# A 90-degree rotation by 128x128 transposes: first loads into the output buffers, narrower macro tiles at both ends

## The chip, the cores and the metric

The kernel runs on one core of one Trainium2 chip. The metric is the device time of one execution in microseconds (us), lower is better; the time before is the median of three runs. Separately, one execution was recorded by the hardware profiler: its page and its trace are what the text reads.

## The reference

```python
"x": np.random.randn(8192, 8192).astype(np.float32), "k": 1
def reference(x, k):
    return np.rot90(x, k)
```

With k = 1 the output is `out[M-1-c, r] = x[r, c]`: each column of the input becomes a row of the output, and the last column becomes the first row. Nothing is computed. 268.4 MB are read and 268.4 MB are written.

## The kernel before, in words

The input is cut into bands of R = 1024 rows (`for r0`), each band into two macro tiles of C = 4096 columns (`widths` returns `[M // 2] * 2`), so there are 16 macro tiles of 16 MB. A macro tile is handled in two stages.

**Load stage.** For each of the 8 row tiles `t` of 128 rows, SyncE's queue (SP) issues one load of 128 rows by 4096 columns, 2 MB, into a buffer `a` (line 82); each partition gets one row piece of 16 KB. The pool of `a` has two buffers. VectorE (DVE) then copies the row tile into eight chunks `ar` of 128x512 (line 89); the copy turns the order of the columns inside each block of 128 around. The pool of `ar` has 68 buffers: one macro tile needs 64 of them, so the next macro tile's copies can take 4 at once and the others as they come free. DVE takes them in the order of the loads, and the buffer `a` can be loaded again when its eight copies are done.

**Store stage.** For each group of G = 4 blocks of 128 columns, which is one chunk column, TensorE (PE) transposes the blocks of all 8 row tiles into PSUM (line 104), two column blocks to a PSUM tile `ps` of 128x2048, of which there are two. ScalarE (ACT) copies each `ps` into one half of an output buffer `o` (line 109), two halves to a buffer, and then issues one store of 2 MB (line 115): 128 partitions of 16 KB, each written as four pieces of 4 KB, one in each of four blocks of 128 output rows. The pool of `o` has two buffers as well. A group can only start when all 8 row tiles of the macro tile have been loaded and copied, since each of its output rows runs over all 1024 input rows of the band.

The engines each go through their instructions in a fixed order, and a framework sets that order and the semaphores. Loads are on SP's DMA queue, stores on ACT's; both queues use the same 16 DMA engines. A step waits for the data and the buffer that it needs, and a DMA also for the earlier one that used the same of eight completion semaphores. `whole_reads`, run at the end of the build, joins a contiguous DMA source that stands as four pieces into one run; it acts on the stores of `o`, and stays as it is.

In the text L0 to L127 are the loads and S0 to S127 the stores, in order. Before, macro tile n has loads and stores 8n to 8n+7.

Of the kernel before, what the change touches and what calls it, by code (L numbers as in the profile page):

```python
# [2 lines left out]

# [5 lines left out]

P = 128  # L10

R = 1024
RT = R // P
CH = 512
G = 4
PW = 2


def whole_reads(nc):

    for fn in nc.m.functions:
        for block in fn.blocks:  # L30
            for n, ins in enumerate(block.instructions):
                if not isinstance(ins, mybir.InstDMACopy):
                    continue
                src = ins.ins[0]
                ap = [list(d) for d in src.ap]
                if len(ap) == 3 and ap[2][0] == 1 and ap[1][0] == ap[2][1]:
                    ap = [ap[0], [1, 1], [1, ap[1][1] * ap[2][1]]]
                    block.instructions[n] = copy.replace(
                        ins,
                        ins=[copy.replace(src, ap=ap)],  # L40
                        ant_dge_precooked=False,
                    )


def widths(first, last, M):

    return [M // 2] * 2


@with_exitstack  # L50
def kernel(
    ctx: ExitStack,
    tc: tile.TileContext,
    x: bass.AP,
    k: bass.AP,
    out: bass.AP,
):
    nc = tc.nc
    assert k == 1, f"only k=1 supported, got {k}"
    nc.at_finalize(whole_reads)  # L60

    N, M = x.shape
    dt = x.dtype

    consts = ctx.enter_context(tc.tile_pool(name="consts", bufs=1))
    ident = consts.tile([P, P], dt)
    make_identity(nc, ident)

    a_pool = ctx.enter_context(tc.tile_pool(name="a_pool", bufs=2))
    r_pool = ctx.enter_context(tc.tile_pool(name="r_pool", bufs=68))  # L70
    o_pool = ctx.enter_context(tc.tile_pool(name="o_pool", bufs=2))
    psum_pool = ctx.enter_context(
        tc.tile_pool(name="psum", bufs=2, space=bass.MemoryType.PSUM)
    )

    for r0 in range(0, N, R):
        c0 = 0
        for C in widths(r0 == 0, r0 + R == N, M):
            chunks = {}
            for t in range(RT):  # L80
                a = a_pool.tile([P, C], dt, tag="a")
                nc.sync.dma_start(  # L82
                    out=a[:], in_=x[r0 + t * P : r0 + (t + 1) * P, c0 : c0 + C]
                )


                for j in range(C // CH):
                    ar = r_pool.tile([P, CH // P, P], dt, tag="ar")
                    nc.vector.tensor_copy(  # L89
                        out=ar[:],  # L90
                        in_=a[:, j * CH : (j + 1) * CH].rearrange(
                            "r (b m) -> r b m", m=P
                        )[:, :, ::-1],
                    )
                    chunks[t, j] = ar

            for g0 in range(0, C // P, G):
                o = o_pool.tile([P, G, R], dt, tag="o")
                for h in range(0, G, PW):
                    ps = psum_pool.tile([P, PW, R], mybir.dt.float32)  # L100
                    for w in range(PW):
                        g = g0 + h + w
                        for t in range(RT):
                            nc.tensor.transpose(  # L104
                                ps[:, PW - 1 - w, t * P : (t + 1) * P],
                                chunks[t, g * P // CH][:, g % (CH // P), :],
                                ident,
                            )
                    nc.scalar.copy(o[:, G - PW - h : G - h, :], ps[:])  # L109

                top = M - c0 - (g0 + G) * P
                dst = out[top : top + G * P, r0 : r0 + R].rearrange(
                    "(g m) f -> m g f", g=G
                )
                nc.scalar.dma_start(out=dst, in_=o[:])  # L115
            c0 += C


# [1 line left out]
_INS = ['x', 'k']  # L120
_OUTS = [((8192, 8192), 'float32')]

_NUMBERS = {'k': 1}


# [26 lines left out]
```

## Time and profile before

| | |
|---|---|
| median of 3 runs | 1278.4 us (1276.62 to 1279.38) |
| the profiled execution's own time | 1282.29 us |
| its span, first to last instruction | 1280.5 us |
| PE busy | 720.3 us, 56% |
| ACT busy | 467.0 us, 36% |
| DVE busy | 355.2 us, 28% |
| DMA over the span | 537.55 MB, 420 GB/s on average |
| loads (line 82) | 128 of 2048 KB, 16.6 us from issue to landing |
| stores (line 115) | 128 of 2048 KB, 15.9 us from issue to landing |

The page cuts the span into 40 slices of 32 us; a digit in it is the busy share in tenths, and the row GB/s what the DMA engines moved. "Idle before" in the list of groups is the time in which an engine waited just ahead of that instruction, with what ended the wait. The chain is the work that ended last, followed back from the end. The profiled execution took 3.9 us more than the median of the runs.

### The profile page before, as it was taken

What the parts mean: (1) busy time and instruction counts of PE and PEld (TensorE: products, weight loads), DVE (VectorE), ACT (ScalarE), POOL (GpSimd) and SP (SyncE); (2) the same over time, 40 slices, a digit from 0 to 9 for tenths busy, and PEclk for the clock granted to TensorE, in tenths of its full rate; (3) what the DMA queues carried; (4) which work ended last, traced back from release to release, by engine and by line L of the source; (5) the groups of instructions that cost most, each with busy time, mean ns of one, the idle gap of its engine ahead of it and who ended that gap; (6) DMA issues with size and microseconds to landing.
All of it is one profiled execution on the core that took longest, in us unless ns stands there. A gap on an engine that the chain in (4) does not pass through costs nothing.

```text
span 1280.5 us, 10385 instructions
## 1 busy us (share of the span) xinstructions
PE 720.3 (56%) x4096; PEld 686.7 (54%) x4096; DVE 355.2 (28%) x1024; ACT 467.0 (36%) x257; POOL 0.7 (0%) x6
## 2 busy tenths in 40 slices
PE   0445555655665456565655655656556655655574
PEld 0345555655555456555555654555555645555474
DVE  3432223222322232233223222322232223222300
ACT  0233334333333343343334333433343334333455
POOL 0000000000000000000000000000000000000000
PEclk9967867687777877768677677686776777787778
DMA  9999999999999999999999999999999999999988
GB/s 346 364 421 425 426 426 424 429 429 428 429 430 427 430 425 431 425 431 427 426 428 429 430 422 426 428 428 426 429 429 424 425 426 426 428 426 427 427 352 357
DMA packets 36913, 537.55 MB, mean 420 GB/s; under 512 B 4096, under 2 KB 4096, under 8 KB 4096
## 3 DMA queue, kind: packets, MB, share of 16 engines
q1 hardware_dynamic: 18432, 268.44, 49.9%
q10 hardware_dynamic: 18432, 268.44, 49.4%
q8 instruction: 32, 0.52, 0.2%
q14 instruction: 17, 0.14, 0.0%
HBM read 268.44 MB, written 268.44 MB: 419 GB/s over the span
## 4 chain that ended last, share of the span: by engine, by line
DMA 79%; ACT 18%; PE 1%; DVE 1%; issue 1%; ACTq 0%; SPq 0%
DMA out_dram<-o 76%; ACT o L109 18%; DMA a<-in_x_dram 3%; PE ps L104 1%; DVE ar L89 1%; ACTq L115 0%; ACTq L109 0%; SPq L82 0%
## 5 line engine op out<-in xcount | busy, mean ns | idle before, releaser
L104 PE MATMUL ps<-ident,ar 128*128 128x128 f32 x4096 | 720.3, 358 | 548.6 <-ACT o L109 502.3
L104 PEld LDWEIGHTS ps<-ident,ar 128*128 128x128 f32 x4096 | 686.7, 192 | 581.9 <-ACT o L109 532.6
L109 ACT COPY o<-ps 128x2048 f32<-128x2048 f32 x256 | 465.7, 1871 | 805.3 <-DMA out_dram<-o 750.7
L89 DVE COPY ar<-a 128x512 f32<-128x512 f32 x1024 | 355.2, 422 | 871.5 <-DMA a<-in_x_dram 871.5
L109 ACT ACT_TABLE_LOAD x1 | 1.3, 1283 | 0.7 <-PEq L133 0.7
masks.py:199 POOL TENSOR_SCALAR_AFFINE_SELECT ident<-ident 128x128 f32<-128x128 f32 x1 | 0.3, 293 | 0.1
masks.py:197 POOL MEMSET ident<- 128x128 f32 x1 | 0.2, 204 | 0.3 <-POOLq L133 0.3
L133 POOL MEMSET const-bfloat16-1.0<- 128x1 bf16 x1 | 0.1, 101 | 0.0
L133 POOL MEMSET const-uint8-127<- 128x1 uint8 x1 | 0.1, 101 | 0.0
L133 POOL MEMSET const-float32-0.0<- 128x1 f32 x1 | 0.1, 98 | 0.2 <-issue 0.2
L133 POOL MEMSET const-float32-1.0<- 128x1 f32 x1 | 0.1, 98 | 0.0
## 6 DMA issues: line engine op xcount, KB each, us to landing
a<-in_x_dram SPq DMA_DIRECT2D x128, 2048.0 KB, 16.6
out_dram<-o ACTq DMA_DIRECT2D x128, 2048.0 KB, 15.9
```

Of the source, the lines that this page charges most:

```text
L89: nc.vector.tensor_copy(out=ar[:], in_=a[:, j * CH : (j + 1) * CH].rearrange("r (b m) -> r b m", m=P)[:, :, ::-1],)
L104: nc.tensor.transpose(ps[:, PW - 1 - w, t * P : (t + 1) * P], chunks[t, g * P // CH][:, g % (CH // P), :], ident,)
L109: nc.scalar.copy(o[:, G - PW - h : G - h, :], ps[:])
L133: nc = _bacc.Bacc("TRN2", target_bir_lowering=False, num_devices=1)
```

## The change

1. The macro tiles are made by `macro_tiles`. The widths stay 4096 except in two places: the first macro tile of the first band becomes three of 1024, 1024 and 2048 columns, and the last of the last band becomes three of 2048, 1024 and 1024 columns.
2. A load stays 2 MB: for a macro tile of width C it takes q = 4096 // C row tiles at once, so that each partition gets q row pieces of C elements (4 of 4 KB for C = 1024, 2 of 8 KB for C = 2048). DVE's copies go through the row tiles of a load, and inside each through its chunks; their number and shapes are the same.
3. The first two loads, L0 and L1, take their buffers from the pool of `o` in place of that of `a`. They are the whole first macro tile of 1024 columns. SP so issues four loads ahead of its first wait, and a wait for DVE's copies stands ahead of the first eviction into each of those two buffers.
4. The last group of the last macro tile stores each half, 1 MB, after its own eviction; all other groups store 2 MB as before.

The stores have the same shape and the same groups of four blocks otherwise. SP's loads become 4 of 4x1024, 4 of 2x2048, 112 of 4096, 4 of 2x2048 and 4 of 4x1024 elements per partition; the counts of PE's, DVE's and ACT's compute instructions don't change.

```diff
-def widths(first, last, M):
-
-    return [M // 2] * 2
+def macro_tiles(N, M):
+
+    for r0 in range(0, N, R):
+        widths = [W] * (M // W)
+        if r0 == 0:
+            widths[:1] = [1024, 1024, 2048]
+        if r0 + R == N:
+            widths[-1:] = [2048, 1024, 1024]
+        c0 = 0
+        for C in widths:
+            yield r0, c0, C
+            c0 += C
...
-            for t in range(RT):
-                a = a_pool.tile([P, C], dt, tag="a")
-                nc.sync.dma_start(
-                    out=a[:], in_=x[r0 + t * P : r0 + (t + 1) * P, c0 : c0 + C]
-                )
+        q = W // C
+        chunks = {}
+        for t0 in range(0, RT, q):
+            if loads < 2:
+                a = o_pool.tile([P, W], dt, tag="o")
+            else:
+                a = a_pool.tile([P, W], dt, tag="a")
+            loads += 1
+            a = a.rearrange("r (q c) -> r q c", q=q)
+            nc.sync.dma_start(
+                out=a,
+                in_=x[r0 + t0 * P : r0 + (t0 + q) * P, c0 : c0 + C].rearrange(
+                    "(q r) c -> r q c", q=q
+                ),
+            )
+            for u in range(q):
                 for j in range(C // CH):
...
-                        in_=a[:, j * CH : (j + 1) * CH].rearrange(
+                        in_=a[:, u, j * CH : (j + 1) * CH].rearrange(
...
-                    chunks[t, j] = ar
+                    chunks[t0 + u, j] = ar
...
+            S = PW if last and g0 + G == C // P else G
...
+                done = h + PW
+                if done % S == 0:
+                    top = M - c0 - (g0 + done) * P
+                    dst = out[top : top + S * P, r0 : r0 + R].rearrange(
+                        "(g m) f -> m g f", g=S
+                    )
+                    nc.scalar.dma_start(
+                        out=dst, in_=o[:, G - done : G - done + S, :]
+                    )
```

More of the change, by code (lines that the diff above doesn't have):

```diff
@@ L16 @@
 RT = R // P
+W = 4096
 CH = 512
@@ L74 @@
     )
[L76 to L79, printed above, removed]
-            for t in range(RT):
-                a = a_pool.tile([P, C], dt, tag="a")
-                nc.sync.dma_start(
-                    out=a[:], in_=x[r0 + t * P : r0 + (t + 1) * P, c0 : c0 + C]
-                )
+    tiles = list(macro_tiles(N, M))
+    loads = 0
+    for r0, c0, C in tiles:
+        last = (r0, c0, C) == tiles[-1]
+        q = W // C
[14 more added lines that the diff above has]
+            for u in range(q):
                 for j in range(C // CH):
@@ L94 @@
                     )
-                    chunks[t, j] = ar
[L97 to L116, printed above, removed]
+                    chunks[t0 + u, j] = ar
+        for g0 in range(0, C // P, G):
+            ot = o_pool.tile([P, W], dt, tag="o")
+            o = ot.rearrange("m (g f) -> m g f", g=G)
+            S = PW if last and g0 + G == C // P else G
+            for h in range(0, G, PW):
+                ps = psum_pool.tile([P, PW, R], mybir.dt.float32)
+                for w in range(PW):
+                    g = g0 + h + w
+                    for t in range(RT):
+                        nc.tensor.transpose(
+                            ps[:, PW - 1 - w, t * P : (t + 1) * P],
+                            chunks[t, g * P // CH][:, g % (CH // P), :],
+                            ident,
+                        )
+                nc.scalar.copy(o[:, G - PW - h : G - h, :], ps[:])
+                done = h + PW
[6 more added lines that the diff above has]
+                        out=dst, in_=o[:, G - done : G - done + S, :]
+                    )
 _INS = ['x', 'k']
```

## The prediction

> **What bounds the kernel now.** I read the page's slices and chain first, then the busy table by stage, then the order of time at both ends.
>
> ```profile
> DMA  9999999999999999999999999999999999999988
> GB/s 346 364 421 425 426 426 424 429 429 428 429 430 427 430 425 431 425 431 427 426 428 429 430 422 426 428 428 426 429 429 424 425 426 426 428 426 427 427 352 357
> ...
> DMA 79%; ACT 18%; PE 1%; DVE 1%; issue 1%; ACTq 0%; SPq 0%
> ```
>
> The DMA engines are full everywhere, and no compute engine is over 56% busy. In the middle they move 427 GB/s; only the first two and last two slices of 32 us fall to about 355. So the middle is at its limit, and only the ends can be won. The table by stage (us, busy by engine, clock, DMA share, GB/s) puts sizes on that:
>
> ```profile
> 0.00:3.00 3.00, 0.00 (x0) 0.00 (x0) 0.00 (x0) 1.28 (x1) 0.70 (x6) 1.00 0.43 98
> 3.00:12.00 9.00, 0.66 (x2) 0.29 (x2) 2.77 (x8) 0.00 (x0) 0.00 (x0) 1.00 1.01 431
> 12.00:50.00 38.00, 4.14 (x12) 1.74 (x12) 16.65 (x48) 0.00 (x0) 0.00 (x0) 1.00 0.92 338
> ...
> 500.00:1220.00 720.00, 417.12 (x2345) 399.78 (x2344) 202.60 (x584) 265.46 (x146) 0.00 (x0) 0.75 1.01 427
> 1224.00:1234.00 10.00, 8.15 (x51) 7.92 (x52) 2.70 (x8) 7.09 (x4) 0.00 (x0) 0.67 0.62 264
> 1234.00:1270.00 36.00, 25.71 (x208) 23.85 (x205) 0.00 (x0) 22.45 (x13) 0.00 (x0) 0.95 0.89 375
> 1270.00:1280.50 10.50, 0.00 (x0) 0.00 (x0) 0.00 (x0) 3.00 (x2) 0.00 (x0) 0.57 0.75 317
> ```
>
> Each stage loses its length times (1 - rate/427). Front: 2.3 us before data flows, 7.9 in 12 to 50, about 1 more up to 80. Back: 3.8 + 4.4 + 2.7 = 10.9. Some 22 us in all, no more than that is in reach. Note 3 to 12: with two loads queued, loads alone reach 431. From 12 on each new load waits for a buffer to land and be copied. DVE's copies, in order of time, are the landings:
>
> ```profile
> 8.18 2.77 DVE L89 COPY ar<-a 128x512 f32<-128x512 f32 x8 [8.18 <-DMA a<-in_x_dram]
> ...
> 13.05 2.77 DVE L89 COPY ar<-a 128x512 f32<-128x512 f32 x8 [2.09 <-DMA a<-in_x_dram]
> ...
> 50.54 2.77 DVE L89 COPY ar<-a 128x512 f32<-128x512 f32 x8 [2.65 <-DMA a<-in_x_dram]
> ```
>
> The second load lands 4.87 us after the first, the next six need (50.54 - 13.05)/6 = 6.25 us each. At 427 GB/s a 2 MB transfer costs 4.91. A load with no store beside it, in the two-buffer rhythm, wastes about 1.38 us. At the other end the last seven stores are issued from 1237.97 to 1273.03, 5.84 us apart: 0.93 wasted each.
>
> **What the skill says.** (1) "DMA: Bandwidth & Descriptors", Issuing engines are not separate DMA queues: SP's and ACT's transfers share the same 16 engines. The trace agrees: mixed, each queue gets a transfer through every 9.8 us, half rate. (2) Same page, Queues, rings and completion order: an engine takes turns between queues packet by packet. The trace has whole 16 KB rows on the load side and equal shares; it can't show turns with 4 KB pieces. (3) Same page, Why small descriptors are slow: about 3 cycles per packet on beats of 32 B. (4) Same page, Latency and other measured facts: large power-of-two row pitches can cost HBM copies half their rate. The stores already write pieces 4 MiB apart (128 rows of 32 KB), within a mix at 427.
>
> **The change, part by part.**
>
> *Four loads at the start.* SP issues L0 to L3 without a wait. DMA keeps the 427 GB/s of the deep queue until about 2.3 + 4 x 4.91 = 22 us, in place of 12. Two more loads at 4.87 in place of 6.25: **-2.8 us**. The added waits: ACT's first eviction into each output buffer waits for DVE's copies of L0 and L1 (done about 11.0 and 15.8); behind that wait are only ACT's table load, 1.3 us, and evictions that have no data before 15.5. Nothing is late.
>
> *Narrow macro tiles in front.* S0 needs L0 and L1 only. Before, the last chunk it needed was ready at 50.98 and S0 was issued at 57.06, 6.1 later. Now that chunk is the seventh copy of L1, 13.05 + 7 x 0.35 = 15.5, so S0 is issued at about 21.6, 35 us sooner. But that is not 35 us won. A 4096-wide tile needs eight loads landed before its first store; in a mix, loads and stores go one to one, so the lead of loads over stores has to grow from 2 (first tile) through 4 to 8, in stretches with loads alone. My walk, at 9.8 per pair: S0 to S3 mix with L4 to L7 from 23 to 62; L7's copies and the 6.1 us path put S4's data at about 73, so 62 to 73 is loads alone (L8, most of L9); S4 to S7 mix until about 112; then loads alone to L15's landing at about 126, and S8 is issued at about 132.5. From there it is the old kernel at 57.06 with eight pairs done. Eight pairs at 9.83 (110 evictions from 142.69 to 1223.72) are 78.6, so the old S0 corresponds to 135.7: about 3.2 gained, the four-load part included. By count: before, 2 fast loads and 7 slow ones alone; now 4 fast ones, and about 5 slow. The first load of each new stretch alone may already be queued and so go at 4.9: at most 2 x 1.38 more. On the low side, if stores get the larger share against narrow loads, S3 is done 9 us sooner and two more loads stand alone: 2 x 1.38 less. I take **-3.0** for the front, range -0.2 to -5.8.
>
> *Narrow macro tiles at the back.* In the last band loads run eight ahead already, since that is what the tile before needs. L127 lands at about 1223.9, and S120's first eviction at 1229.35 waits for PE, whose transposes start at 1225.64 because ACT released a PSUM tile at 1225.6, not because of L127's chunk (ready about 1224.4). A tile that needs fewer loads so releases nothing: **0**. If narrow loads lag behind stores, the mix lasts longer and up to four of the last stores run at 4.91 instead of 5.84: 4 x 0.93 = 3.7 gained; if they lag so far that a store group waits for its loads, one 6.1 us path is exposed. Both ends go to the range.
>
> *Split last store.* The last 2 MB store is issued at 1273.03. Its first half could be issued about 1.9 us (one eviction) sooner. The one before, issued at 1266.89, fills the engines until about 1271.8 to 1273.5 (shortest issue to landing 6.6, of which 4.9 is data), so only the gap of about 1.7 between it and the last one's first packet can close; the extra issue on ACT holds the second eviction up 0.7. **-1.0**, between 0 and -2.4.
>
> *Narrow loads.* Sixteen of 128. By (3), 16 KB in four packets takes 4 x 131 cycles against 515, 1.7%; in two, 0.6%: at 4.91 each, 8 x 0.083 + 8 x 0.03 = 0.9, an estimate. The stores with their 4 KB pieces hold 427 beside loads, and up to 419 alone. **+0.4**, from 0 to 0.9, except as in the third rival. SP's issue, 0.33, may become the 0.55 that the four-piece stores take: hidden behind 5 us and more of queued data.
>
> Sum: -3.0 + 0 - 1.0 + 0.4 = **-3.6 us**. The profiled execution of 1282.3 would become 1278.7, its span 1276.9; from the median of 1278.4, **1274.8**.
>
> **The rivals.**
>
> *More is won at the back (1270.3).* Turns by packet let stores run ahead of narrow loads; the lead falls before loads end, and four store-only transfers join the mix (-3.7), with the gap at 1224 to 1234 partly filled (-0.8). For it: 264 GB/s there. Against: the equal halves of the trace, and a 4 KB-piece store counted like a 16 KB load.
>
> *The stretch is only moved (1277.4).* The lead of eight must be built anyway. If stores take the larger share in front, the two loads gained stand alone later, and only the split is left: -1.0.
>
> *Slower: reads of pieces 4 MiB apart (1286.8).* If reads suffer from that pitch as (4) tells, at its 164 against 214 GB/s a 4.91 us load takes 1.5 more; eight loads of four pieces make +12 against -3.6, about +8.4. It decides against me from (3.6 + 2.6)/16 = 0.4 us per narrow load. Against: the stores' same pattern at full rate, and neighbouring partitions only 32 KB apart. That the change doesn't do what it says is excluded: the order of instructions has four loads ahead of SP's first wait.
>
> **How the numbers follow.** 0.2% is 2.6 us, about what a measurement of this kernel tells from no change. Forecast 0.53 (1272 to 1277.5), more at the back 0.14, only moved 0.22, slower reads 0.11. Faster by over 0.2%: most of the forecast (0.47), the first rival (0.14), little of the second (0.02): 0.63. Slower: 0.11. Same: 0.26. The range leaves out the slow rival and the far end of the first: 1270.0 to 1279.5, where the upper end is the second rival with half of the narrow loads' and the share's cost on top.
>
> **What would show it.** Landings of L0 to L3 about 4.9 apart; the first store issued near 21.6; two stretches of loads alone near 62 to 73 and 112 to 135 at about 340 GB/s; S8 issued near 132.5; the last seven full stores still some 5.8 apart; 427 GB/s in between. Wrong it would be if L2 and L3 land over 5.5 apart (narrow reads cost), if S0 to S3 take well under 9.8 each beside narrow loads (turns by packet), or if stores at the end go faster than 5.8 apart.

## The result and the profile after

The changed kernel took 1277.56 us (median of 4 runs, 1276.9 to 1278.14) beside 1278.89 for the kernel before: a ratio of 0.9993 with a 95% interval of 0.9975 to 1.001. That is 0.9 us faster, from 3.2 faster to 1.3 slower. Measured once more with 21 runs, the unaltered changed kernel came to 1278.06 beside 1279.98, ratio 0.9986 (0.9979 to 0.9993): 1.8 us faster, and clear of zero. The forecast was 3.6 us. Its sign held, its size was twice what was found.

The profiled executions differ by more than that: spans of 1280.5 before and 1275.1 after. Single executions of one kernel scatter by some us here (1276.19 to 1283.31 in 37 runs of the kernel before), and the profiled one of before (1282.29) lies 2.0 to 3.9 above the medians of its sets of runs. So the traces are read for where time goes within one execution, and the runs for how much it is.

The slices of the changed kernel's page, with its DMA packets:

```profile
DMA  9999999999999999999999999999999999999998
GB/s 362 427 403 399 421 422 425 429 430 429 428 429 430 429 429 420 428 429 430 427 428 430 431 427 429 427 426 429 427 430 428 428 425 430 426 424 424 420 408 340
DMA packets 41153, 537.55 MB, mean 422 GB/s; under 512 B 4112, under 2 KB 4112, under 8 KB 8208
```

Before, the second slice had 364; now it has 427, but the third and fourth fell to 403 and 399, which were at 421 and 425. The loss was moved and spread as well as cut. And 4096 packets of 2 to 8 KB are new: eight narrow loads of 4x1024 elements, each cut into 512 packets of 4 KB.

The busy table of the changed kernel by finer stages (us, busy by engine, clock, DMA share, GB/s):

```profile
3.00:20.00 17.00, 8.34 (x32) 5.51 (x32) 6.83 (x20) 2.96 (x2) 0.00 (x0) 1.00 1.02 411
...
23.00:26.00 3.00, 2.18 (x16) 1.52 (x14) 2.17 (x7) 3.00 (x2) 0.00 (x0) 1.00 1.03 302
26.00:30.00 4.00, 2.95 (x25) 2.71 (x25) 0.60 (x2) 0.39 (x1) 0.00 (x0) 1.00 0.99 356
30.00:58.00 28.00, 7.01 (x36) 6.16 (x36) 5.55 (x16) 7.27 (x4) 0.00 (x0) 0.67 1.01 429
...
62.00:66.00 4.00, 0.54 (x2) 0.25 (x3) 1.82 (x6) 0.00 (x0) 0.00 (x0) 0.50 0.90 326
...
114.00:134.00 20.00, 8.42 (x43) 7.07 (x43) 9.45 (x28) 3.73 (x2) 0.00 (x0) 0.55 0.93 378
```

Against 428 GB/s, each line loses its length times (1 - rate/428): 0.7 us at the start, where narrow loads go at 411 with full engines (wide ones went at 431); 0.9 + 0.7 from 23 to 30, around the first store; nothing in the mix of 30 to 58; 1.0 and 2.3 in the two stretches of loads alone. With what lies between, and 2.5 before data flows, the front loses about 9.4 us; before it was 11.2.

DVE's copies of the changed kernel in order of time are the landings of L1 to L7:

```profile
13.61 2.77 DVE L111 COPY ar<-a 128x512 f32<-128x512 f32 x8 [2.34 <-DMA a<-in_x_dram]
18.72 2.77 DVE L111 COPY ar<-a 128x512 f32<-128x512 f32 x8 [2.34 <-DMA a<-in_x_dram]
23.82 2.77 DVE L111 COPY ar<-a 128x512 f32<-128x512 f32 x8 [2.33 <-DMA a<-in_x_dram]
35.12 2.77 DVE L111 COPY ar<-a 128x512 f32<-128x512 f32 x8 [8.52 <-DMA a<-in_x_dram]
47.68 2.77 DVE L111 COPY ar<-a 128x512 f32<-128x512 f32 x8 [9.78 <-DMA a<-in_x_dram]
60.50 2.77 DVE L111 COPY ar<-a 128x512 f32<-128x512 f32 x8 [10.05 <-DMA a<-in_x_dram]
65.45 2.77 DVE L111 COPY ar<-a 128x512 f32<-128x512 f32 x8 [2.18 <-DMA a<-in_x_dram]
```

ACT's evictions in the same stretch show when S0 and S1 had landed (the first two lines: each waits for a store), and when S4 and S8 could start and were issued:

```profile
36.71 3.63 ACT L133 COPY ot<-ps 128x2048 f32<-128x2048 f32 x2 [10.32 <-DMA out_dram<-ot]
...
44.32 3.64 ACT L133 COPY ot<-ps 128x2048 f32<-128x2048 f32 x2 [3.98 <-DMA out_dram<-ot]
...
69.50 3.76 ACT L133 COPY ot<-ps 128x2048 f32<-128x2048 f32 x2 [21.54 <-PE ps L128]
73.28 0.55 ACTq L141 DMA_DIRECT2D out_dram<-ot  x1
...
130.20 3.79 ACT L133 COPY ot<-ps 128x2048 f32<-128x2048 f32 x2 [31.03 <-PE ps L128]
134.01 0.55 ACTq L141 DMA_DIRECT2D out_dram<-ot  x1
```

L0 to L3 land 5.1 apart (forecast 4.9). Beside the stores, L5 and L6 need 12.6 and 12.8 us while the two stores land 7.6 apart; equal halves would be 9.8 each. A third of the engines would be 3 x 4.91 = 14.7, two thirds 7.4. S4 was issued at 73.28 (the forecast's first stretch of loads alone ended at about 73), S8 at 134.01 (forecast 132.5).

The last band. Before, DVE's copies for L126 and L127, the last two in order of time:

```profile
1214.13 2.77 DVE L89 COPY ar<-a 128x512 f32<-128x512 f32 x8 [7.07 <-DMA a<-in_x_dram]
1223.92 2.77 DVE L89 COPY ar<-a 128x512 f32<-128x512 f32 x8 [7.02 <-DMA a<-in_x_dram]
```

In the changed kernel, the landings of L124 to L127:

```profile
1206.42 2.78 DVE L111 COPY ar<-a 128x512 f32<-128x512 f32 x8 [7.09 <-DMA a<-in_x_dram]
1214.55 2.77 DVE L111 COPY ar<-a 128x512 f32<-128x512 f32 x8 [5.35 <-DMA a<-in_x_dram]
1232.91 2.77 DVE L111 COPY ar<-a 128x512 f32<-128x512 f32 x8 [15.59 <-DMA a<-in_x_dram]
1249.48 2.77 DVE L111 COPY ar<-a 128x512 f32<-128x512 f32 x8 [13.80 <-DMA a<-in_x_dram]
```

ACT's evictions and issues there, in order of time, from the eviction for S118 on:

```profile
1196.33 3.64 ACT L133 COPY ot<-ps 128x2048 f32<-128x2048 f32 x2 [3.88 <-DMA out_dram<-ot]
1206.40 0.55 ACTq L141 DMA_DIRECT2D out_dram<-ot  x1
1207.05 3.63 ACT L133 COPY ot<-ps 128x2048 f32<-128x2048 f32 x2 [7.07 <-DMA a<-in_x_dram]
```

L126 and L127 need 18.4 and 16.6 us; before, every load took 9.8, and L127 landed at 1223.92, with S119 to S127 still to be issued. Now only S124 to S127 are issued after it. But S118, evicted at 1199.97, is issued at 1206.40, just as L124 lands: in the trace both carry the same completion semaphore, number 109. For 6.4 us a finished store stood behind a load that the stores themselves held up.

### The profile page after: what moved, and what is told of

It is laid out like the page before. It is cut to its first block, busy times and chain, and to the rows that moved or that the text cites. A ratio compares the mean times of both kernels' runs of the same rounds, so it can differ in the third digit from the quotient of the medians.

```text
span 1275.1 us, 10403 instructions
## 1 busy us (share of the span) xinstructions
PE 719.3 (56%) x4096; PEld 681.8 (53%) x4096; DVE 355.2 (28%) x1024; ACT 467.1 (37%) x257; POOL 0.7 (0%) x6
## 2 busy tenths in 40 slices
DMA packets 41153, 537.55 MB, mean 422 GB/s; under 512 B 4112, under 2 KB 4112, under 8 KB 8208
## 4 chain that ended last, share of the span: by engine, by line
DMA 84%; DVE 12%; issue 2%; ACT 1%; PE 1%; DVEq 0%; SPq 0%; ACTq 0%
DMA a<-in_x_dram 81%; DVE ar L111 12%; DMA out_dram<-ot 3%; ACT ot L133 1%; PE ps L128 1%; DVEq L111 0%; SPq L100 0%; ACTq L133 0%; ACTq L141 0%
## 5 line engine op out<-in xcount | busy, mean ns | idle before, releaser
L133 ACT COPY ot<-ps 128x2048 f32<-128x2048 f32 x256 | 465.9, 1870 | 789.5 <-DMA out_dram<-ot 715.2
## 6 DMA issues: line engine op xcount, KB each, us to landing
a<-in_x_dram SPq DMA_DIRECT2D x128, 2048.0 KB, 16.6
```

## The experiments

The theory formed from the trace: the engines take turns by packet. A whole load and a store both go as 16 KB packets and share equally; a narrow load goes as 8 or 4 KB packets and gets a third or a fifth beside stores. So in front stores finish early and loads stand alone afterwards (the second rival of the prediction), and at the back loads are drawn out. The rival: equal shares, and two profiles that differ by chance.

The traces show the shares directly. They hold a record of every packet, with its queue, size, start and length. Summed over stretches in which both queues were at work (the last two are of a kernel described below, with four stores cut into 4 KB packets):

| kernel, stretch in us | packets of loads, of stores | loads, stores in GB/s | share of the loads |
|---|---|---|---|
| before, 500 to 1220 | 16 KB, 16 KB | 213, 213 | 0.50 |
| changed, 30 to 39 | 8 KB, 16 KB | 141, 285 | 0.33 |
| changed, 1216 to 1221 | 4 KB, 16 KB | 82, 339 | 0.19 |
| four stores cut, 46 to 53 | 8 KB, 4 KB | 282, 145 | 0.66 |
| four stores cut, 62 to 65 | 16 KB, 4 KB | 343, 87 | 0.80 |

One packet from each queue in turn would give 0.50, 0.33, 0.20, 0.67 and 0.80. So the turns by packet are shown; what they cost in time is for the runs. Ratios are to the kernel before, with 95% intervals.

**The front alone.** The last macro tile stays 4096 wide, the last store whole.

```diff
-            widths[-1:] = [2048, 1024, 1024]
+            pass
...
-            S = PW if last and g0 + G == C // P else G
+            S = G
```

> The changed kernel with the last macro tile 4096 wide and its last store whole: only the front of the change is left. Theory (turns by packet: narrow loads go as 4 or 8 KB packets and get a fifth or a third of the engines beside 16 KB store packets, so part of the front's gain is given back): S8 issued at 134.0 as in the changed kernel, which is 1.6 us ahead of the kernel before (135.7); from L119's landing to the end 135 us as before; in all about 1.6 us faster than before. Rival (the front gains what was predicted, and the changed kernel's trace has a slow front by accident): S8 at 132.5, 3 us faster. Rival (the ends gain nothing, the two profiles differ by chance): S8 at 135.7 or later.

Measured: 0.9996 (0.9989 to 1.0002), 0.5 us faster and not told from none. S8 was issued at 133.77. By the place of S8 the theory's 134.0 held, and the predicted 132.5 did not. But the 134.0 had been read from the changed kernel, so this shows that the front runs the same way again, and not why; and the 1.6 us that the theory put on it lie outside the interval (1.4 us faster to 0.3 slower).

**The back alone.** The first macro tile stays 4096 wide and all loads use their own pool.

```diff
-            widths[:1] = [1024, 1024, 2048]
+            pass
...
-            if loads < 2:
+            if loads < 0:
```

> The kernel before with only the last macro tile divided and the last store split. Theory (turns by packet: stores run ahead of the narrow loads, so the mix lasts longer): S0 issued at 57.1 as before; from L119's landing to the end 132.4 us as in the changed kernel, against 135.2 before; about 2.8 us faster. Rival (a tile that needs fewer loads releases nothing, only the split counts, as the prediction had it): 134.2 us, 1.0 faster, and the last loads land one for one with the stores, 9.8 us apart.

Measured: 0.9994 (0.9985 to 1.0002), 0.8 us faster, not told from none. From L119's landing (1144.90) to the end of the span (1276.5) it took 131.6 us, and the last loads were drawn out as in the changed kernel: the mechanism is there, the 2.8 us aren't in the runs.

**The split alone.** As the back alone, with the last macro tile left 4096 wide too, so that only the last store is cut.

```diff
-            widths[-1:] = [2048, 1024, 1024]
+            pass
```

> The kernel before with only the last 2 MB store cut into two of 1 MB. By the prediction: the first half's packets follow those of the store before without a gap, 1.0 us off the end; from L119's landing to the end 134.2 us. Rival (the split is the back's whole gain): 132.4 us, 2.8 off. Rival (the second half's issue and landing eat it up): 135.2.

Measured: 0.9995 (0.9987 to 1.0003), 0.6 us faster, not told from none and near the 1.0 of the prediction; 134.5 us from L119's landing to the end.

**The early pair alone.** Only L0 and L1 go into the output buffers; all macro tiles are 4096 wide, the last store is whole.

```diff
-            widths[:1] = [1024, 1024, 2048]
+            pass
...
-            widths[-1:] = [2048, 1024, 1024]
+            pass
...
-            S = PW if last and g0 + G == C // P else G
+            S = G
```

> The kernel before with only L0 and L1 in the output buffers, so that four wide loads are queued at the start; all macro tiles 4096 wide. By the prediction's first step: L0 to L3 land 4.9 us apart, the later ones 6.25, S0 issued at 57.1 - 2.8 = 54.3, 2.8 us faster. Rival (the two-buffer rhythm only sets in later and the fast loads are paid for by a longer gap before L4): S0 at 56 to 57, 0 to 1 us faster.

Measured: 0.9973 (0.996 to 0.9986), 3.5 us faster (1.8 to 5.1). Its landings in order of time, L1 to L4 and L7:

```profile
12.91 2.77 DVE L111 COPY ar<-a 128x512 f32<-128x512 f32 x8 [2.12 <-DMA a<-in_x_dram]
17.80 2.77 DVE L111 COPY ar<-a 128x512 f32<-128x512 f32 x8 [2.12 <-DMA a<-in_x_dram]
22.70 2.77 DVE L111 COPY ar<-a 128x512 f32<-128x512 f32 x8 [2.12 <-DMA a<-in_x_dram]
29.98 2.77 DVE L111 COPY ar<-a 128x512 f32<-128x512 f32 x8 [4.51 <-DMA a<-in_x_dram]
...
47.83 2.44 DVE L111 COPY ar<-a 128x512 f32<-128x512 f32 x7 [2.14 <-DMA a<-in_x_dram]
```

4.9 apart up to L3, then (47.83 - 22.70)/4 = 6.3; S0 was issued at 54.34 against 57.06, 2.7 sooner. The first step of the prediction is right, by itself. One of the four parts of the change gained more here than the whole did.

**Pair and back, without the narrow front.**

```diff
-            widths[:1] = [1024, 1024, 2048]
+            pass
```

> L0 and L1 in the output buffers, the first macro tile left 4096 wide, the last one divided and the last store split: the two parts that gained so far (3.5 and about 0.8 us by their runs), without the narrow front. If the parts add, 4.3 us faster than before, about 1275.8 where before is 1280.1; S0 issued at 54.3, from L119's landing to the end about 132. If the narrow front is what the changed kernel loses by, this beats the changed kernel by about 3 us. Rival (the runs of the first call differ by chance, and the narrow front costs nothing): within 1 us of the changed kernel.

Measured: 0.9969 (0.9958 to 0.998), 4.0 us faster. That fits the 4.3 to which the parts add up. It is 2.2 us more than the 1.8 of the changed kernel; the two ratios come from different sets of runs, and their intervals touch.

**The narrow front without the pair.** As the front alone, and L0 and L1 in their own pool.

```diff
-            if loads < 2:
+            if loads < 0:
```

> The first macro tile divided into 1024, 1024, 2048, but all loads in the two buffers of their own pool; the back as before. Theory (turns by packet and three starts of the stores cost about 3 us against the wide first tile): 0 to 3 us slower than the kernel before, the store stretch of S0 to S3 ends about 10 us before L7 lands, S8 issued near 137. Rival (dividing the first tile is neutral or helps by itself, as the prediction's walk has it: 5 slow loads alone in place of 7): S8 at 134 to 135, 1 to 2 us faster than before.

Measured: 0.9994 (0.9986 to 1.0002), 0.8 us faster, not told from none. S8 was issued at 133.85: the theory's 137 did not occur, and the rival's 134 to 135 came near. The surprise is that taking the pair away cost nothing that the runs can tell. Its L1 to L3:

```profile
13.29 2.77 DVE L111 COPY ar<-a 128x512 f32<-128x512 f32 x8 [2.33 <-DMA a<-in_x_dram]
18.54 2.78 DVE L111 COPY ar<-a 128x512 f32<-128x512 f32 x8 [2.48 <-DMA a<-in_x_dram]
23.72 2.44 DVE L111 COPY ar<-a 128x512 f32<-128x512 f32 x7 [2.40 <-DMA a<-in_x_dram]
```

With two buffers narrow loads already land 5.2 apart, where wide ones needed 6.25; with four queued they land 5.1 apart. The pair has nothing to save there. So its 2.8 and the narrow tiles' gain don't add. Why narrow loads hardly suffer from the two-buffer rhythm was not taken further. Their width isn't all of it: L13 to L16 of the changed kernel are wide and have no store beside them from 115.5 on, and their copies start at 117.39, 122.24, 127.50 and 132.87, also some 5.2 apart.

**Eight stores cut.** The changed kernel, but S0 to S7 keep their source in four pieces, so that they go as 4 KB packets.

```diff
+    stores = 0
...
                 ap = [list(d) for d in src.ap]
+                cut = False
+                if ins.engine == mybir.EngineType.Activation:
+                    stores += 1
+                    cut = stores <= 8
+                if cut:
+                    continue
```

> The changed kernel, but S0 to S7 keep their source as four pieces of 4 KB; all else as in the changed kernel. Theory (turns by packet): beside these stores a narrow load of 8 KB packets now gets two thirds of the engines in place of one third, a wide one four fifths in place of a half, so the loads build up their lead inside the mix, stretches of loads alone become short, L7 lands near 53 instead of 65, and S8 is issued near 128 instead of 134: up to 5 us faster than the changed kernel. Rival (shares go by bytes or by what is queued): L7 near 65, S8 at 134 to 135, 0 to 1 us slower for the smaller packets.

Measured: 0.9959 (0.9947 to 0.9971), 5.2 us faster. L7 landed at 55.1, near what the turns give (53), not at 65. But S8 was issued at 137.85, not near 128: S6, issued at 108.09, shared with whole loads, got about a fifth, and only at 134.19 was its buffer free. The shares overshot: first loads too late, now stores. That S8 came later than in the changed kernel and the whole is still faster is no contradiction, since more loads had landed by then: from 62 to 134 the DMA moved 426 GB/s in place of 403, which is 3.9 us of data.

**All stores cut, nothing else.** The kernel before with all stores as four pieces.

```diff
-    nc.at_finalize(whole_reads)
```

> The kernel before without the joining of the stores' sources: all 128 stores go as four pieces of 4 KB, the loads stay whole. It prices small packets and tests the turns alone, with no change to tiles. Theory (turns by packet): beside a store a load gets four fifths, so loads land about 8 to 9 us after issue in place of 16.6, and wait for the chunks; a store's 2 MB cost 4 to 6% more as L0 to L3 of the changed kernel did (5.1 against 4.9 us apart), 128 x 0.2 = 26 us slower in all. Rival (equal shares by bytes): loads still 16 to 17 us from issue to landing, and the time within 5 us.

Measured, with two runs: 1.0382 (1.0356 to 1.0408), 49 us slower. From its page, the loads' copies and the DMA issues:

```profile
L88 DVE COPY ar<-a 128x512 f32<-128x512 f32 x1024 | 362.5, 422 | 908.3 <-PE ps L103 746.9
...
a<-in_x_dram SPq DMA_DIRECT2D x128, 2048.0 KB, 10.7
out_dram<-o ACTq DMA_DIRECT2D x128, 2048.0 KB, 16.6
```

Loads land in 10.7 us in place of 16.6, and then DVE waits for PE to free chunks, 746.9 us in all where it had waited for loads. No tile was changed. The 16 to 17 us of equal shares did not occur, but the theory's 8 to 9 were missed as well, and a load that is alone in its queue would land sooner than in 16 at equal shares too; the packets in the table above are the better witness. The price was mis-sized, 26 against 49 us: from 500 to 1100 the DMA ran at 410 GB/s in place of 427, which over the whole kernel is an estimated 53 us. In the packet records one of 4 KB took 159 ns and one of 16 KB 611, so half the bytes in 4 KB packets are about 2%, the expected 26 us. With eight stores cut, whole loads and 4 KB stores ran at 425 from 56 to 120. Where the rest is lost isn't shown.

**Four stores cut.** As with eight, and only for S0 to S3, which stand beside narrow loads and L8 on.

```diff
-                    cut = stores <= 8
+                    cut = stores <= 4
```

> The changed kernel, but S0 to S3 alone keep their source as four pieces of 4 KB; S4 on go whole. With eight stores cut the loads took so much that S8 came only at 137.8, with the DMA at 344 GB/s from 137 to 143. Theory (turns by packet): with four cut, L7 still lands near 55, S4 to S7 get their half again beside wide loads, S8 is issued near 125 to 130, and the total is at least as good as with eight cut, ratio 0.994 to 0.996. Rival (the gain of the eight cut stores came from elsewhere than the shares of S0 to S3): ratio 0.998 to 1.000, as the changed kernel.

Measured: 0.9939 (0.9925 to 0.9953), 1271.74 us: 7.8 us faster than before, the best of all. S8 was issued at 125.92. Its busy table:

```profile
3.00:22.00 19.00, 10.75 (x50) 7.66 (x51) 8.32 (x24) 5.02 (x3) 0.00 (x0) 1.00 1.02 411
22.00:56.00 34.00, 12.39 (x80) 11.25 (x79) 12.51 (x37) 7.27 (x4) 0.00 (x0) 0.72 1.02 411
56.00:90.00 34.00, 11.12 (x64) 10.25 (x64) 14.71 (x44) 7.27 (x4) 0.00 (x0) 0.70 1.01 428
90.00:120.00 30.00, 16.66 (x96) 15.61 (x96) 8.85 (x26) 11.00 (x6) 0.00 (x0) 0.69 1.01 429
120.00:140.00 20.00, 12.07 (x64) 11.75 (x64) 5.55 (x16) 7.27 (x4) 0.00 (x0) 0.66 1.01 429
```

From 56 to 140 there is no stretch of loads alone left. In the changed kernel those stretches lost 1.0 + 2.3 us and some more around them: from 62 to 134 it moved 403 GB/s and this kernel 428, 4.2 us of data. L4 to L7 land at 32.06, 39.53, 47.10 and 54.59, some 7.5 apart: 4.91 x 1.5, two thirds of the engines, as 8 KB packets beside 4 KB ones get in the table.

**The changed kernel again.** Beside the same runs of before as the four cut stores and the next.

> The changed kernel once more, unaltered, on the chip and beside the runs of the kernel before that the next two share: its first measurement has four runs and an interval of 4 us. If the narrow front is worth as little in it as in the kernels with that front alone: ratio 0.998 to 0.9995, 0.6 to 2.5 us faster than before. If the prediction's size was right: 0.997, 3.6 us.

Measured: 0.9986 (0.9979 to 0.9993), as told at the start. Four cut stores are 6.0 us ahead of it.

**Pair and split, no narrow load.**

```diff
-            widths[:1] = [1024, 1024, 2048]
+            pass
...
-            widths[-1:] = [2048, 1024, 1024]
+            pass
```

> L0 and L1 in the output buffers and the last store split, all macro tiles 4096 wide: no narrow load is left. Theory (the narrow tiles gain nothing net: their 4 and 8 KB packets move at 405 to 410 GB/s instead of 427, which costs about what the shorter stretches of one-way traffic save): as fast as with the divided last tile, ratio about 0.997, and faster than the changed kernel by 2 to 3 us. Rival (the divided last tile is worth 1 to 2 us by itself): ratio 0.998, slower than that kernel by as much.

Measured: 0.9979 (0.9972 to 0.9986), 2.7 us faster. Half of the interval overlaps that of the changed kernel (0.9979 to 0.9993); the two ratios lie 0.9 us apart, less than the 2 to 3 expected.

**Four cut stores, last macro tile wide.** The best kernel, with only its last store split at the back.

```diff
-            widths[-1:] = [2048, 1024, 1024]
+            pass
```

> The best kernel so far (changed kernel with S0 to S3 as four pieces of 4 KB), but with the last macro tile left 4096 wide; only its last store is split. It prices the divided last tile. Theory (narrow loads at the back prolong the mix but move at 405 to 420 GB/s, and the last store groups then wait for L127; the two cancel): ratio 0.993 to 0.995, within 1.3 us of the kernel with the divided last tile (0.9939); the last loads land one for one with the stores again, L127 near 1217, and the DMA does some 265 GB/s in the ten us after it. Rival (the divided last tile is worth 1.5 us or more): 0.9952 or higher.

Measured: 0.9951 (0.9938 to 0.9965). The divided last tile is worth 1.5 us by this pair, 1.3 by pair and back against pair and split, 0.1 by the back against the split; no one of them is clear of zero. About 1 us is likely, not settled. Its L127 lands at 1217.5, and its busy table has 287 GB/s from 1217 to 1227, where the kernel before had 264 just after its L127.

## Why the prediction had the sign and half the size

- **Four loads at the start, -2.8.** Right by itself: S0 at 54.34 where 54.3 follows, 3.5 us (1.8 to 5.1) in the runs. Wrong as a term of this sum. In narrow loads the two-buffer rhythm costs 5.2 and not 6.25 us a load, so the pair adds nothing to a narrow front (0.9996 with it, 0.9994 without).
- **Narrow macro tiles in front, -3.0 with the pair.** This is the term that was mis-sized. The runs of the front alone show 0.5 us (1.4 faster to 0.3 slower) in place of 3.0. The packet records allow a second reading: at 300 us, the bytes moved lag behind a DMA that runs at 428 GB/s from the start by 12.1 to 12.9 us in the three kernels with the old front (before, back alone, split alone), by 10.5 to 11.2 in the three executions with this front (changed, changed again, front alone), and by 8.5 to 9.8 in the three with only the pair in front (early pair, pair and back, pair and split). By that the front gains 1.8 us and the pair alone 3.3, so the narrow tiles on top of the pair cost some 1.5. Between 0.5 and 1.8 it stays open which is nearer.
- **What failed in its walk.** It assumed one load per store in the mix; the shares went by packet. S0 to S3 were done early, L7 landed at 65.45 and not at 62, and loads stood alone from about 59. The prediction had that as its second rival, with 2 x 1.38 as its price, and set it at 0.22. But the next time of the walk came out all the same: S4 was issued at 73.28 for 73, since it took 7.8 us from L7's landing where the walk had 11. Loads alone were even dearer in the walk: its five slow ones are 6.9 us, and from 62 to 134 the changed kernel lost 4.2. What the walk left out stands at the start: 0.8 us for narrow loads at 411 GB/s and 1.6 from 23 to 30, together 2.4 against the 0.4 that was allowed. So the shares are shown, but not that they alone made S8 1.5 us late. No run had narrow loads beside stores with packets of the same size, which would separate the two.
- **What the shares are worth.** With nothing changed but the packets of four stores, which gives the loads the larger share, loads no longer stand alone, and 6.0 us come off. The lag at 300 us, between 10.5 and 11.2 with this front, is 4.7 with four stores cut, which says the same.
- **Narrow macro tiles at the back, 0.** The reason given, that a tile which needs fewer loads releases nothing, was half of it: the shares did change, L127 came 26 us later and fewer stores ran alone, which was the first rival. But the gap was moved more than filled: 315 GB/s from 1242 to 1253, around L127's landing, lose 2.9 us, where 264 from 1224 to 1234 had lost 3.8. S118's wait cost little by itself (419 GB/s from 1197 to 1207). About 1 us is left, not settled.
- **Split, -1.0.** 0.6 (1.7 faster to 0.4 slower): right within what can be told.
- **Narrow loads, +0.4.** The rate of 411 at the start costs 0.8 us over 20 us, near the upper bound of 0.9 for all sixteen: four 4 KB packets took 4 x 159 ns against 611 for one of 16 KB, 4% more, and not the 1.7% that the estimate under (3) gave. In the front's mix they cost nothing: 429 from 30 to 58. At the back the rate was 407 from 1200 to 1234, with S118's wait in it. The third rival, reads of pieces 4 MiB apart at a fraction of the rate, did not occur (L0 to L3 5.1 us apart). Its price had taken the 164 GB/s that the page under (4) gives for a pitch of 2 MiB; for 4 MiB it gives 103.

The prediction had named the right sign of being wrong: S0 to S3 "well under 9.8 each beside narrow loads" was seen (7.6 us apart). The Trainium skill, "DMA: Bandwidth & Descriptors", Queues, rings and completion order, says that an engine switches queues at packet boundaries; the runs agree (loads of 8 KB packets had a third beside stores of 16 KB, and L5 took 12.6 us against the stores' 7.6). The prediction set that page aside for the equal halves of the trace before, and counted a store there as 4 KB pieces. The page of before says otherwise:

```profile
DMA packets 36913, 537.55 MB, mean 420 GB/s; under 512 B 4096, under 2 KB 4096, under 8 KB 4096
```

No packet lies between 512 B and 8 KB, and the 537.55 MB in the other 32817 packets are about 16 KB each. So the stores too went as 16 KB packets, and the equal halves said nothing against turns by packet.

## What to carry to other kernels

Here, with both DMA queues full, the size of their packets set their shares (a third for 8 KB beside 16 KB, a fifth for 4 KB), so a transfer that was cut into pieces fell behind one that wasn't; look at both access patterns, and at the page's packet sizes, before counting on one for one. That can be used: cut the side that should wait, and keep whole the side that the next stage waits for, but only as long as it should. And gains at one end of a kernel don't add when they remove the same idle time: try each part alone, since here one of four parts was worth as much as all of them or more.

## What was not expected of the hardware

- Loads in a two-buffer rhythm with no store beside them landed 6.25 us apart at the start of the kernel before as 16 KB rows, and 5.2 apart as four pieces of 4 KB, although with four queued the smaller packets are the slower ones (5.1 against 4.9). The wide L13 to L16 of the changed kernel landed some 5.2 apart as well. This isn't explained.
- Eight cut stores gave 5.2 us and four gave 7.8; all 128 cost 49.
- From 23 to 30, where loads turn from 4 KB to 8 KB packets and the first store starts, the engines move 302 and 356 GB/s with a share of 1.03 and 0.99: busy, but slow. The packets of S0 come only from 26.6 on, so the store isn't all of it; the load packets of 8 KB took over 500 ns from 25 to 27, and 309 from 30 on. The kernel with four cut stores has this dip too (322 and 368), and it isn't explained.
